# Choosing the 256 keys of sparse attention from the sign of score less threshold, on ScalarE

## The chip, the cores and the metric

The kernel runs on one core of a Trainium2 chip. The metric is device time in microseconds of one execution. The core has five engines that each work through a queue of their own in order: TensorE (PE, matmuls; PEld is its weight load), VectorE (DVE), ScalarE (ACT), GpSimd (POOL) and SyncE (SP, which issues DMA).

## The reference

Two layers, each with gated linear attention (4 heads) and sparse attention (8 heads) over 1040 tokens of width 1024. What matters here is the choice of keys:

```python
score = jnp.einsum('bqj,bqjs->bqs', iwb * (IDX_HEADS ** -0.5), jax.nn.relu(dots))
causal = key_pos[None, :] <= t[:, None]
score = jnp.where(causal[None], score, -jnp.inf)
_, sel = lax.top_k(score, topk)                    # topk = 256
...
s = jnp.where(valid[:, :, None, None, :], s, -jnp.inf)
p = jax.nn.softmax(s, axis=-1)
```

Each query keeps the 256 causal keys with the highest score. Of keys whose score equals the lowest one kept, those that come first are kept.

## The kernel before, in words

The kernel gathers no keys. It holds scores for a block of 128 queries on 128 partitions, in tiles `score[i]` for blocks 1 to 7 that are W = 144 + 128 i columns wide: 272, 400, 528, 656, 784, 912 and 1040, together 4592. Block 0 has at most 144 keys and needs no choice. For each query it finds the value of the 256th key (`sel_v`, one column for each block). From it, it makes a tile `bias[i]` in bfloat16 (in `r_kb`), 0 for a kept key and very large for any other, which L1023 adds to the attention scores S as it reads them from PSUM; the exponential (L1029, ScalarE) then follows.

The part that is changed (`cnt = er[0]` and the loop behind it) stands once in each layer's code. For each block, DVE counts the scores above the threshold (L866, with a sum in `cnt`), marks those equal to it (L867), runs a scan that numbers the equal ones from count - 256 on (L868), keeps the mark where the number is above 0, so that the place is too many (L870), and adds the scores below the threshold (L871). GpSimd multiplies by 1e30 (L872) and adds the causal mask for the last 128 columns (L873). The search for the threshold ends in a branch (L826 to L853) that all engines wait for and that is a longer search for rare cases.

Around the selection TensorE computes the gates of the two attentions, eight projections `proj_z` in three tiles of 348, 346 and 346 tokens. A tile is a group of 24 matmuls (L353 to L355, `wz`) into one PSUM bank. It is finished by three ScalarE passes (L404 to L406), one DVE pass (L731), an exponential (L732, ScalarE) and a product on DVE (L737) that is the last to read the bank and so frees it. Just behind the branch the values are transposed (L885, `vT`) and split into a high and a low part (`va`, `vb`: L887 ScalarE, L888 DVE), and the attention's keys `ak` are split likewise (L896, then L897). Then `stage_a` makes S (L1022, 144 columns for block 0, 272 for block 1), reads it (L1023) and takes the exponential; `stage_b` transposes the result (L1047, L1057) and multiplies by the values (L1053, L1054, L1063). Blocks 0 and 1 of this attention need no late `bias` tile, or only `bias[1]`; the others follow.

No queue is written by hand in full: a scheduler orders the instructions of each engine by a simulated time line when the program is built. So a change of one stage can move others.

Of the kernel before, what the change touches and what calls it, by code (L numbers as in the profile page):

```python
# [13 lines left out]
U8 = mybir.dt.uint8  # L14
U16 = mybir.dt.uint16
I16 = mybir.dt.int16
BF16 = mybir.dt.bfloat16
AF = mybir.ActivationFunctionType
OP = mybir.AluOpType
# [11 lines left out]
BIG = 1e30  # L31
# [65 lines left out]
def trunk(ctx: ExitStack, tc, a, out, dbg=None, stop=None):  # L97
# [58 lines left out]
    def small(n, dt=F32, parts=1):  # L156
        o = cofs[0]
        cofs[0] = o + n
        assert cofs[0] <= CST
        return cst[:, o:o + n].bitcast(dt) if dt != F32 else cst[:, o:o + n]  # L160
# [19 lines left out]
    V.memset(halves, 0.0)  # L180
    for o in range(2):
        V.memset(halves[64 * o:64 * o + 64, o:o + 1], 1.0)
    zcol = small(2)
    V.memset(zcol[:, 0:1], 0.0)
    V.memset(zcol[:, 1:2], 1.0)
    zero_b = zcol[:, 0:1]
# [222 lines left out]
    for l in range(DEPTH):  # L409
# [380 lines left out]
        with tc.high_priority(offset=TPRI):  # L790
# [65 lines left out]
                    V.drain()  # L856
                    finish(cnt, V.drain)

            cnt = er[0]
            for i in blks:  # L860
                W = 144 + 128 * i
                t = sel_v[:, i - 1:i]
                rr[5] = 1 - rr[5]
                oz = r_oz[:, rr[5]]
                eq, cs = oz[:, :260].bitcast(U8), oz[:, 260:780].bitcast(I16)
                V.tensor_scalar(bias[i], score[i], t, float(-TOPK), OP.is_gt, OP.add, accum_out=cnt[:, i - 1:i])  # L866
                V.tensor_scalar(eq[:, :W], score[i], t, None, OP.is_equal)  # L867
                V.tensor_tensor_scan(cs[:, :W], eq[:, :W], zero_b.to_broadcast([128, W]), cnt[:, i - 1:i],  # L868
                                     OP.add, OP.add)
                V.scalar_tensor_tensor(eq[:, :W], cs[:, :W], 0.0, eq[:, :W], OP.is_gt, OP.mult)  # L870
                V.scalar_tensor_tensor(score[i], score[i], t, eq[:, :W], OP.is_lt, OP.add)  # L871
                G.tensor_scalar(bias[i], score[i], BIG, 0.0, OP.mult, OP.add)  # L872
                G.tensor_tensor(bias[i][:, W - 128:W], bias[i][:, W - 128:W], causal[:, 16:144], OP.add)  # L873

        vat = [slot(1, F32R, "va"), slot(3, F32R, "vb")]
        va = []
# [305 lines left out]
def _tables():  # L1182
# [24 lines left out]
    for p in range(128):  # L1207
        for i in range(1, NB):
            nv = 17 + 128 * i + p
            z = NormalDist().inv_cdf(max(5e-3, 1 - TOPK / nv))  # L1210
            seltab[p, i - 1] = z
            seltab[p, 6 + i] = np.sqrt(2 * np.pi) / (nv * max(np.exp(-z * z / 2), 0.15))
            seltab[p, 13 + i] = BIG if nv >= TOPK else -BIG
            seltab[p, 20 + i] = nv >= TOPK
    seltab[:, 28:] = np.arange(8) + 0.5
    return {"ident": np.eye(128, dtype=np.float32), "causal": causal, "mcaus": mcaus, "lmask": lmask,
# [43 lines left out]
```

## Time and profile before

| | |
|---|---|
| median of 3 runs | 1513.29 us (1512.71 to 1514.68) |
| the profiled execution, whole | 1515.28 us |
| its span, first to last instruction | 1513.5 us |
| TensorE busy | 1386.8 us (92%) |
| DVE busy | 1061.5 us (70%) |
| ScalarE busy | 762.6 us (50%) |
| GpSimd busy | 723.3 us (48%) |
| mean granted TensorE clock | 0.965 |

The span is the profiled execution without what lies before its first and behind its last instruction, 1.8 us. Busy shares are averages over stages that have different limits; TensorE's matmuls are pipelined, so that its busy time is not its work at full speed. The granted clock is a share of 2.4 GHz; TensorE runs at this or at 1.2 GHz.

### The profile page before, as it was taken

The numbers are of one execution on the slowest core, as the hardware profiler recorded it, in microseconds if no ns is written. First come the engines' busy times: TensorE is split into PE (matmuls) and PEld (weight loads), VectorE is DVE, ScalarE is ACT, GpSimd is POOL, SyncE is SP. The second block draws the span as 40 slices with busy tenths as digits, with TensorE's granted clock in tenths as the row PEclk, the third lists the DMA queues.
The fourth block names the chain that finished last, engine by engine and source line by source line (L and its number), as shares of the span: only waits on it lengthen the run. The fifth ranks groups of instructions, "written<-read, shape, count | busy, mean of one in ns | idle before, by whom it ended". The sixth has DMA issues, their size and how long they took to land. (4 is left out here: it accounts for less than half of the span.)

```text
span 1513.5 us, 27140 instructions
## 1 busy us (share of the span) xinstructions
PE 1386.8 (92%) x9471; PEld 1290.6 (85%) x9471; DVE 1061.5 (70%) x2465; ACT 762.6 (50%) x1745; POOL 723.3 (48%) x690
## 2 busy tenths in 40 slices
PE   2988998999968999999999899999997899999985
PEld 2888897898958998898998889888897799899985
DVE  8569999565197556776497699994624955778638
ACT  5446623343355777653254573334434577876412
POOL 6533346596344546322363442866923644652134
PEclk9999999999978999999999999999998899999988
DMA  7242331242423446215233432314242253631422
GB/s 250 102 141 82 91 116 50 86 127 83 129 64 92 136 132 163 66 48 158 75 126 116 124 98 81 107 58 127 83 131 64 65 147 106 183 109 52 153 67 112
DMA packets 143166, 162.63 MB, mean 107 GB/s; under 512 B 19552, under 2 KB 112496, under 8 KB 143024
## 3 DMA queue, kind: packets, MB, share of 16 engines
q1 hardware_dynamic: 112656, 125.73, 27.9%
q10 hardware_dynamic: 30368, 35.12, 6.8%
q8 instruction: 75, 1.23, 0.3%
q14 instruction: 67, 0.55, 0.1%
HBM read 104.76 MB, written 56.04 MB: 106 GB/s over the span
## 5 line engine op out<-in xcount | busy, mean ns | idle before, releaser
L320 POOL TENSOR_TENSOR w<-w 128x512 fp32r<-128x512 f32 (+1 forms) x134 | 179.4, 1339 | 299.6 <-ACT w L319 232.5
L319 ACT ACTIVATE w<-w 128x512 fp32r<-128x512 f32 (+1 forms) x134 | 83.4, 624 | 108.7 <-DMA w<-in_w_fm_dram 58.4
L353 PE MATMUL wz<-X,w 128*128 128x346 f32 (+1 forms) x384 | 130.5, 340 | 2.3 <-DVE zu L737 1.8
L540 DVE SCALAR_TENSOR_TENSOR r_sc<-v,cst,r_sc 128x346 f32<-128x346 f32 (+6 forms) x196 | 125.0, 693 | 6.3 <-ACT v L535 5.2
L354 PE MATMUL wz<-X,w 128*128 128x346 f32 (+1 forms) x384 | 129.3, 337 | 0.0
L355 PE MATMUL wz<-X,w 128*128 128x346 f32 (+1 forms) x384 | 129.3, 337 | 0.0
L1051 DVE TENSOR_TENSOR u<-PT,u 128x512 fp32r<-128x512 f32 (+1 forms) x160 | 100.4, 632 | 30.1 <-ACT u L1050 21.3
L1050 ACT ACTIVATE u<-PT 128x512 fp32r<-128x512 f32 (+1 forms) x160 | 85.9, 544 | 61.9 <-PE PT L1047 60.4
L1029 ACT ACTIVATE r_g<-r_g,cst 128x272 f32<-128x272 f32 (+7 forms) x128 | 99.7, 779 | 20.1 <-DVE cst L1023 19.8
L632 POOL TENSOR_TENSOR qb<-r_g,u 64x256 f32<-64x256 f32 (+1 forms) x144 | 104.2, 724 | 5.8
L1022 PE MATMUL S<-ak,aq 128*128 128x346 f32 (+7 forms) x240 | 81.9, 348 | 18.8 <-DVE ak L897 10.3
L567 PE MATMUL gvp<-w,X 128*128 128x256 f32 (+1 forms) x288 | 83.3, 291 | 9.5 <-DVE r_g L643 8.0
L535 ACT ACTIVATE v<-dots 128x346 f32<-128x346 f32 (+5 forms) x224 | 85.8, 457 | 12.2 <-PE dots L533 8.5
L1047 PE MATMUL PT<-cst,r_g 128*128 128x128 f32 x576 | 89.2, 278 | 1.1 <-DVE cst L1023 1.1
L568 PE MATMUL gvp<-w,X 128*128 128x256 f32 (+1 forms) x288 | 83.4, 290 | 0.0
L569 PE MATMUL gvp<-w,X 128*128 128x256 f32 (+1 forms) x288 | 82.8, 288 | 0.0
L353 PEld LDWEIGHTS wz<-X,w 128*128 128x128 f32 x384 | 76.4, 199 | 3.9 <-DVE zu L737 2.3
L354 PEld LDWEIGHTS wz<-X,w 128*128 128x128 f32 x384 | 76.7, 200 | 0.3
L355 PEld LDWEIGHTS wz<-X,w 128*128 128x128 f32 x384 | 76.4, 199 | 0.4
L1117 PE MATMUL yp<-w,X 128*128 128x256 f32 (+1 forms) x238 | 69.9, 295 | 6.0 <-ACT X L1087 6.0
L643 DVE COPY_PREDICATED r_g<-cst,lev 128x512 f32<-128x512 uint8 (+1 forms) x72 | 52.5, 729 | 32.0 <-PE lev L639 31.4
L1022 PE MATMUL S<-ak 128*128 128x346 f32 (+7 forms) x240 | 74.8, 320 | 0.0
(348 smaller groups left out, 4900.6 us busy)
## 6 DMA issues: line engine op xcount, KB each, us to landing
w<-in_w_fm_dram SPq DMA_DIRECT2D x88, 256.0 KB
r_g<-aq_dram SPq DMA_DIRECT2D x64, 128.0 KB
w<-in_w_out_dram SPq DMA_DIRECT2D x32, 256.0 KB
r_sc<-h_dram SPq DMA_DIRECT2D x53, 128.0 KB
h_dram<-r_g SPq DMA_DIRECT2D x12, 512.0 KB
r_dram<-r_sc SPq DMA_DIRECT2D x48, 128.0 KB
r_sc<-z_dram SPq DMA_DIRECT2D x22, 256.0 KB
z_dram<-zu ACTq DMA_DIRECT2D x32, 173.0 KB
```

The source lines that it names most:

```text
L320: G.tensor_tensor(lo[:, :n], raw[:, :n], hi[:, :n].bitcast(F32), OP.subtract)
L353: T.matmul(p[:m, :n], wh, xh, start=(k == 0), stop=False)
L354: T.matmul(p[:m, :n], wh, xl, start=False, stop=False)
L355: mm = T.matmul(p[:m, :n], wl, xh, start=False, stop=(k == 7))
L535: S.activation(rl[:, :n], p[:, :n], AF.Relu)
L540: V.scalar_tensor_tensor(sco[:, c:c + n], rl[:, :n], w, sco[:, c:c + n], OP.mult, OP.add)
L632: eng.tensor_tensor(qb[P, :, o].rearrange("p c (b m) -> p c b m", m=m), qv[P, :, 1, :].rearrange("p (c b) m -> p c b m", c=nch), Ev[P, :, ...
L1022: mm = T.matmul(p[:, :n], q[x][:, h % 4, :], ak[g][:, c:c + n], start=(x == 0), stop=(x == 1))
L1029: ins = S.activation(P[:, :W], P[:, :W], AF.Exp, bias=mx[:, h, nci - 1:nci], scale=-1.0, accum_out=mx[:, h, 4:5]).ins
L1047: T.transpose(p[:, 256 * x + 128 * hh:256 * x + 128 * hh + 128], Pt[hh][:, 128 * (k0 + x):128 * (k0 + x) + 128], ident)
L1050: S.activation(ph[:, :256 * kk], p[:, :256 * kk], AF.Copy)
L1051: V.tensor_tensor(pl[:, :256 * kk], p[:, :256 * kk], ph[:, :256 * kk].bitcast(F32), OP.subtract)
```

## The change

ScalarE now takes the sign of score - threshold (`sg`, +1, 0 or -1, L867 of the new file) with its sum, and its square (`ne`, 1 where the score is not the threshold, L868) with its sum. The two sums give the number of keys above the threshold, and so the room for equal ones (`room`, two DVE operations on one column, L870 and L871). A scan on DVE counts the room down by one at each equal key (L872), 2048 times the sign is added (L873), and ScalarE's Relu with the scale -1e30 makes the bias (L874): a kept key ends at 0, any other far above it. The thresholds of queries with fewer than 256 keys are half as far from zero as before, so that masked scores stay below them, and the causal mask is not added any more. Scans and marks are held in 16 bits where they were in 8 and 16.

```diff
--- before.py
+++ after.py
@@ -180,7 +180,8 @@
     V.memset(halves, 0.0)
     for o in range(2):
         V.memset(halves[64 * o:64 * o + 64, o:o + 1], 1.0)
-    zcol = small(2)
+    zcol = small(3)
+    V.memset(zcol[:, 2:3], -1.0)
     V.memset(zcol[:, 0:1], 0.0)
     V.memset(zcol[:, 1:2], 1.0)
     zero_b = zcol[:, 0:1]
@@ -856,21 +857,21 @@
                     V.drain()
                     finish(cnt, V.drain)
 
-            cnt = er[0]
+            negt, sums, room = sel_w[10], sel_w[8:10], sel_w[7]
+            V.tensor_scalar(negt, sel_v, -1.0, BIG / 2, OP.mult, OP.min)
             for i in blks:
-                W = 144 + 128 * i
-                t = sel_v[:, i - 1:i]
+                W, x = 144 + 128 * i, slice(i - 1, i)
                 rr[5] = 1 - rr[5]
-                oz = r_oz[:, rr[5]]
-                eq, cs = oz[:, :260].bitcast(U8), oz[:, 260:780].bitcast(I16)
-                V.tensor_scalar(bias[i], score[i], t, float(-TOPK), OP.is_gt, OP.add, accum_out=cnt[:, i - 1:i])
-                V.tensor_scalar(eq[:, :W], score[i], t, None, OP.is_equal)
-                V.tensor_tensor_scan(cs[:, :W], eq[:, :W], zero_b.to_broadcast([128, W]), cnt[:, i - 1:i],
-                                     OP.add, OP.add)
-                V.scalar_tensor_tensor(eq[:, :W], cs[:, :W], 0.0, eq[:, :W], OP.is_gt, OP.mult)
-                V.scalar_tensor_tensor(score[i], score[i], t, eq[:, :W], OP.is_lt, OP.add)
-                G.tensor_scalar(bias[i], score[i], BIG, 0.0, OP.mult, OP.add)
-                G.tensor_tensor(bias[i][:, W - 128:W], bias[i][:, W - 128:W], causal[:, 16:144], OP.add)
+                sg, oz = bias[i], r_oz[:, rr[5]]
+                left, ne = oz[:, :520].bitcast(I16), oz[:, 520:].bitcast(BF16)[:, :W]
+                S.activation(sg, score[i], AF.Sign, bias=negt[:, x], scale=1.0, accum_out=sums[0][:, x])
+                S.activation(ne, sg, AF.Square, accum_out=sums[1][:, x])
+
+                V.tensor_scalar(room[:, x], sums[0][:, x], sums[1][:, x], -0.5, OP.add, OP.mult)
+                V.tensor_scalar(room[:, x], room[:, x], float(TOPK), None, OP.add)
+                V.tensor_tensor_scan(left[:, :W], ne, zcol[:, 2:3].to_broadcast([128, W]), room[:, x], OP.add, OP.add)
+                V.scalar_tensor_tensor(left[:, :W], sg, 2048.0, left[:, :W], OP.mult, OP.add)
+                S.activation(bias[i], left[:, :W], AF.Relu, scale=-BIG)
 
         vat = [slot(1, F32R, "va"), slot(3, F32R, "vb")]
         va = []
@@ -1210,7 +1211,7 @@
             z = NormalDist().inv_cdf(max(5e-3, 1 - TOPK / nv))
             seltab[p, i - 1] = z
             seltab[p, 6 + i] = np.sqrt(2 * np.pi) / (nv * max(np.exp(-z * z / 2), 0.15))
-            seltab[p, 13 + i] = BIG if nv >= TOPK else -BIG
+            seltab[p, 13 + i] = BIG if nv >= TOPK else -BIG / 2
             seltab[p, 20 + i] = nv >= TOPK
     seltab[:, 28:] = np.arange(8) + 0.5
     return {"ident": np.eye(128, dtype=np.float32), "causal": causal, "mcaus": mcaus, "lmask": lmask,
```

**The built order.** Names are those of the tiles, out<-in, with sizes; lines of the new file are one higher than those of the old one from line 184 on. In ScalarE's queue of the first layer, this is what stands right behind the branch before, from the last pass of the z tile in hand to the weights, values and keys:

```order
L406 ACTIVATE zu<-zu,cst 128x348
L404 ACTIVATE zu<-wz 128x346
L405 ACTIVATE zu<-zu 128x346
L406 ACTIVATE zu<-zu,cst 128x346
L319 ACTIVATE w<-w 128x512
L887 ACTIVATE va<-vT 128x8x64
L887 ACTIVATE va<-vT 128x2x64
L887 ACTIVATE vb<-vT 128x6x64
L887 ACTIVATE vb<-vT 16x2x64
L896 ACTIVATE ak<-r_g 128x1040 x2
L396 ACTIVATE ak<-r_g 128x512 x2
```

Of the new queue, the branch and that z pass are followed by the seven Signs, of which the last two stand here, and by this:

```order
L867 ACTIVATE r_kb,cst<-r_sc,cst 128x912
L867 ACTIVATE r_kb,cst<-r_sc,cst 128x1040
L405 ACTIVATE zu<-wz 128x346
L733 ACTIVATE zu<-zu 128x348
L868 ACTIVATE r_oz,cst<-r_kb 128x272
L868 ACTIVATE r_oz,cst<-r_kb 128x400
L320 ACTIVATE w<-w 128x512
L888 ACTIVATE va<-vT 128x8x64
L888 ACTIVATE va<-vT 128x2x64
L888 ACTIVATE vb<-vT 128x6x64
L888 ACTIVATE vb<-vT 16x2x64
L897 ACTIVATE ak<-r_g 128x1040 x2
```

The Signs and two Squares stand in front of the values and the keys, and the second and third z tiles behind them; the other Squares and the Relus are spread over what follows.

In DVE's queue of the first layer, these rows come first behind the branch before:

```order
L866 TENSOR_SCALAR r_kb,cst<-r_sc,cst 128x272
L867 TENSOR_SCALAR r_oz<-r_sc,cst 128x272
L866 TENSOR_SCALAR r_kb,cst<-r_sc,cst 128x400
L867 TENSOR_SCALAR r_oz<-r_sc,cst 128x400
L866 TENSOR_SCALAR r_kb,cst<-r_sc,cst 128x528
L866 TENSOR_SCALAR r_kb,cst<-r_sc,cst 128x656
L866 TENSOR_SCALAR r_kb,cst<-r_sc,cst 128x784
L866 TENSOR_SCALAR r_kb,cst<-r_sc,cst 128x912
L866 TENSOR_SCALAR r_kb,cst<-r_sc,cst 128x1040
L731 SCALAR_TENSOR_TENSOR zu<-wz,zu 128x348
L868 SCALAR_TENSOR_TENSOR r_oz<-r_oz,cst 128x272
L868 SCALAR_TENSOR_TENSOR r_oz<-r_oz,cst 128x400
```

and these now:

```order
L861 TENSOR_SCALAR cst<-cst 128x7
L732 SCALAR_TENSOR_TENSOR zu<-wz,zu 128x348
L738 TENSOR_TENSOR zu<-wz,zu 128x348
L870 TENSOR_SCALAR cst<-cst 128x1
L871 TENSOR_SCALAR cst<-cst 128x1
L870 TENSOR_SCALAR cst<-cst 128x1
L872 SCALAR_TENSOR_TENSOR r_oz<-r_oz,cst 128x272
L871 TENSOR_SCALAR cst<-cst 128x1
L873 SCALAR_TENSOR_TENSOR r_oz<-r_kb,r_oz 128x272
L872 SCALAR_TENSOR_TENSOR r_oz<-r_oz,cst 128x400
L889 TENSOR_TENSOR va<-vT,va 128x8x64
L889 TENSOR_TENSOR va<-vT,va 128x2x64
```

The seven counts are gone from the front, and the product that frees the first z tile's bank (L737, now L738) has come up from behind the keys to the third place.

In TensorE's queue of the first layer, the first S tiles (numbers tell tiles apart) stand behind the first of the z groups that follow the branch (`wz_5044`) and ahead of the second (`wz_5077`):

```order
L355 MATMUL wz_5044<-X_90,w_5040 128x348
L1022 MATMUL S_4863<-ak_4839,aq_4848 128x144
L1022 MATMUL S_4863<-ak_4839 128x144
L1022 MATMUL S_4868<-ak_4839,aq_4848 128x144
L1022 MATMUL S_4868<-ak_4839 128x144
L1022 MATMUL S_4984<-ak_4839,aq_4848 128x144
L1022 MATMUL S_4984<-ak_4839 128x144
L353 MATMUL wz_5077<-X_90,w_5033 128x346
L354 MATMUL wz_5077<-X_90,w_5033 128x346
```

Now all of the second group, 24 matmuls (`wz_5079`, of which the last stands here), comes before S, and the S tiles of all eight heads come together:

```order
L356 MATMUL wz_5079<-X_91,w_5042 128x346
L1023 MATMUL S_4865<-ak_4841,aq_4850 128x144
L1023 MATMUL S_4870<-ak_4841,aq_4850 128x144
L1023 MATMUL S_4986<-ak_4841,aq_4850 128x144
L1023 MATMUL S_4865<-ak_4841 128x144
L1023 MATMUL S_4870<-ak_4841 128x144
L1023 MATMUL S_4986<-ak_4841 128x144
L1023 MATMUL S_4991<-ak_4841,aq_4850 128x144
L1023 MATMUL S_4991<-ak_4841 128x144
L1023 MATMUL S_5002<-ak_4841,aq_4850 128x144
L1023 MATMUL S_5002<-ak_4841 128x144
```

The second layer has the same order in all three places. The rest of the program differs only in small exchanges between neighbours.

## Rows read from the trace of the kernel before

**Rows 1.** The page's 40 slices: busy tenths of DVE, TensorE's granted clock.

```profile
DVE  8569999565197556776497699994624955778638
...
PEclk9999999999978999999999999999998899999988
```

**Rows 2.** Busy times by stretch: TensorE, weights, DVE, ScalarE, GpSimd, then clock.

```profile
419.20:466.30 47.10, 31.70 (x157) 29.08 (x158) 46.98 (x87) 24.80 (x66) 28.04 (x22) 0.71 0.24 71
1154.40:1200.10 45.70, 33.41 (x157) 31.00 (x158) 43.49 (x82) 24.99 (x66) 24.55 (x20) 0.71 0.24 69
...
430.00:440.00 10.00, 6.54 (x23) 6.37 (x24) 9.94 (x25) 4.08 (x13) 2.68 (x5) 0.50 0.31 101
```

**Rows 3.** TensorE's waits, first layer, 400 to 500: us, times, longest.

```profile
PE S L1022 <- DVE cst L1023: 5.7, 2, 5.1
PE S L1022 <- DVE ak L897: 5.0, 1, 5.0
```

**Rows 4.** TensorE's longest wait, second layer, 1136 to 1236.

```profile
PE S L1022 <- DVE ak L897: 5.3, 1, 5.3
```

**Rows 5.** Groups by line: the selection's passes, both layers (busy us, mean ns).

```profile
L868 DVE TENSOR_TENSOR_SCAN r_oz<-r_oz,cst 128x272 int16<-128x272 uint8 (+6 forms) x14 | 25.6, 1859 | 0.0
...
L870 DVE SCALAR_TENSOR_TENSOR r_oz<-r_oz 128x272 uint8<-128x272 int16 (+6 forms) x14 | 16.2, 1172 | 0.1
...
L871 DVE SCALAR_TENSOR_TENSOR r_sc<-r_sc,cst,r_oz 128x272 f32<-128x272 f32 (+6 forms) x14 | 14.2, 1027 | 0.0
L872 POOL TENSOR_SCALAR r_kb<-r_sc 128x272 bf16<-128x272 f32 (+6 forms) x14 | 12.4, 883 | 35.4 <-DVE r_sc L871 35.0
...
L866 DVE TENSOR_SCALAR_CACHE_REDUCE r_kb<-r_sc,cst 128x272 bf16<-128x272 f32 (+6 forms) x14 | 11.9, 890 | 17.2 <-PE vT L885 9.7 <-DVEq L828 7.5
...
L873 POOL TENSOR_TENSOR r_kb<-r_kb,cst 128x128 bf16<-128x128 bf16 x14 | 10.5, 750 | 1.0
...
L867 DVE TENSOR_SCALAR r_oz<-r_sc,cst 128x272 uint8<-128x272 f32 (+6 forms) x14 | 10.0, 726 | 0.0
```

**Rows 6.** ScalarE's groups by form.

```profile
L1029 ACT ACTIVATE r_g<-r_g,cst 128x1040 f32<-128x1040 f32 x16 | 18.5, 1157 | 2.0 <-DVE cst L1023 2.0
...
L405 ACT ACTIVATE zu<-zu 128x346 f32<-128x346 f32 x32 | 15.5, 486 | 1.1 <-DVE zu L737 0.6
...
L896 ACT ACTIVATE ak<-r_g 128x1040 fp32r<-128x1040 f32 x4 | 4.0, 1054 | 0.0
...
L107 ACT ACT_TABLE_LOAD x1 | 1.3, 1283 | 0.7 <-PEq L1249 0.7
```

**Rows 7.** TensorE's timeline, first layer: start, length, idle before.

```profile
423.53 0.32 PE L353 MATMUL wz<-X,w 128*128 128x348 f32 x1
...
427.20 0.33 PE L355 MATMUL wz<-X,w 128*128 128x348 f32 x1
...
432.54 0.46 PE L1022 MATMUL S<-ak,aq 128*128 128x144 f32 x1 [5.01 <-DVE ak L897]
...
434.99 0.66 PE L353 MATMUL wz<-X,w 128*128 128x346 f32 x1 [0.93 <-DVE zu L737]
...
460.90 0.66 PE L353 MATMUL wz<-X,w 128*128 128x348 f32 x1
...
466.27 0.32 PE L353 MATMUL wz<-X,w 128*128 128x346 f32 x1
```

**Rows 8.** DVE's timeline, first layer: splits of values and of keys.

```profile
429.59 0.87 DVE L888 TENSOR_TENSOR va<-vT,va 128x512 fp32r<-128x512 f32 x2
430.39 0.73 DVE L888 TENSOR_TENSOR vb<-vT,vb 128x384 fp32r<-128x384 f32 x2
431.15 2.39 DVE L897 TENSOR_TENSOR ak<-r_g,ak 64x1040 fp32r<-64x1040 f32 x2
```

**Rows 9.** DVE's groups by form.

```profile
L731 DVE SCALAR_TENSOR_TENSOR zu<-wz,zu 128x346 f32<-128x346 f32 x32 | 16.4, 511 | 11.7 <-ACT zu L406 8.9 <-PE o L1053 2.5
...
L1023 DVE CUSTOM_DVE_ANT_0 r_g<-S,cst 128x144 f32<-128x144 f32 x16 | 4.1, 298 | 0.0
```


## The prediction, made before the changed kernel was run

> **What bounds the kernel now.** I read the 40 slices first. The granted clock of TensorE (PEclk) is 9 tenths or more in nearly every slice, and dips to 7 and 8 in slices 12 and 13, to 8 in 31 and 32, and at the very end [rows 1]. DVE is at 9 in slices 12 and 32, where the two layers select their keys. So I asked for the busy times from the moment when all engines come out of the selection's branch to the end of the fourth group of 24 z matmuls (`wz`) behind it on TensorE's queue: 47.1 us in the first layer (to 466.27 [rows 7]), 45.7 us in the second [rows 2]. In the first, DVE is busy 47.0 of 47.1 us; TensorE only 31.7, at 0.71 of its clock; ScalarE 24.8; GpSimd 28.0. DVE fills this stage and TensorE waits for it. In the slices around it the clock is full, which I read as TensorE setting the pace there; so time gained here is kept unless something else stops it.
>
> The waits of TensorE say for what [rows 3]: 5.7 us for S tiles that the masked score pass (L1023) still had to read, 5.0 us for the split of the attention keys (L897). In the second layer it is 5.3 us for L897 [rows 4]. (There is also a wait at the branch itself, which the change leaves alone.) Each such gap is paid twice: in the 10 us around the 5.0 us gap the granted clock is 0.50 [rows 2], that is 1.2 GHz. A group of 24 z matmuls takes 3.8 us at the full clock (423.53 to the end of the one at 427.20) and 5.4 us when it starts at the low one (460.90 to 466.27) [rows 7].
>
> **What the change removes, adds and moves.** Off DVE, for a layer (half of each line's total) [rows 5]: the counting compare L866 6.0 us, the equality L867 5.0, the product L870 8.1; of L871 7.1 us one pass of the same form stays (`sg` x 2048 + `left`, same widths). The scan L868 stays, 12.8 us. Added are 14 one-column operations and one of seven; no row has such a pair, so they lie between nothing and the 0.3 us of a 144-column L1023 [rows 9]; I take 0.1 each, as they are the smaller kind, 1.5 us in all (0 to 4.5). DVE loses 19.1 - 1.5 = 17.6 of its 47 us. GpSimd loses L872 and L873, 11.5 us a layer; TensorE hardly waits for it here, so I cost that at nothing.
>
> ScalarE gains 21 passes over 4592 columns each. Copying 1040 columns takes 1.054 us and 346 take 0.486, so a column is 0.82 ns and the fixed part 0.20; with a bias column, 1040 take 1.157 us, so 0.30 fixed [rows 6]. Sign: 4592 x 0.82 ns + 7 x 0.30 = 5.9 us. Square and Relu: 3.8 + 7 x 0.20 = 5.2 us each. Together 16.3 us, on an engine that is idle for 22 of 47 us here.
>
> The Trainium skill speaks against such a move: its page "ScalarE: Activation LUTs" (section "Rules for kernel authors") gives relu and products to VectorE, which it calls up to about 3x faster in bf16. By that, Square and Relu would cost a third on DVE, an estimate of 3.4 us in place of 10.4, and the change would overload ScalarE. The rows of this case do not agree: L871 averages 1.03 us where the mean width is 656 columns, 1.6 ns a column [rows 5], against 0.82 for ScalarE [rows 6].
>
> How the sum of busy times turns into time depends on the new order, so I walked the rows of the three queues, from the release of the branch as 0, with L numbers of before.
>
> Keys. ScalarE's queue now has the seven Signs ahead of everything (0.5 to about 6.4), then two z passes (0.49 each), two Squares (1.0), a weight (0.6), the four value copies (some 1.6, as DVE's splits of the same tiles) and only then the two key copies (2.1): done at about 12, with starts that overlap a little. DVE, with its seven counts gone, waits for its first Square until 7.7 and then does two scans (672 of 4592 columns of 12.8 us: 1.9), two passes of L871's kind (1.0), the value splits (0.87 + 0.73) and L897 (2.39 for two, S needs the first) [rows 8]: S can begin at about 13.8, against 432.54 - 419.2 = 13.3 before [rows 7]. No gain there by itself. But the second group of 24, which stood behind the S tiles, and started at 434.99 after another 0.93 us of waiting [rows 7], now stands in front. Its PSUM bank is free at 7.7, when DVE's L737 for the first z tile runs, which came just before 434.99. It fills 8.3 (427.5, where the first group ends before) to 12.1 at full clock, and the gap shrinks from 5.0 to about 2 us.
>
> Third group. From its last L897 at 15.0, DVE does eight L1023 at 0.3, the scans of 528 and 656 columns (3.3), two L871-like passes (1.8), three z passes at 0.51 [rows 9] and some 0.5 of small ones: L737 frees this group's bank at 24.5. ScalarE must have done some 38 passes by then: 12 z passes 5.9 us, seven Signs 5.9, four Squares 2.3, two Relus 0.95, six of 512 columns 3.7, key copies 2.1, value copies 1.6, five exponentials 2.1, end to end 24.5, and since consecutive passes overlap a little, 21 to 24. It is close behind DVE, no further. [...]
>
> Fourth group. DVE goes on with a 272-column L1023 (somewhat over 0.3, 0.4), scans of 784 and 912 (4.7), two passes (2.6), z passes (1.0), the small ones and two remainder passes (1.3): 34.5. That also covers the bank of the fourth group. The attention matmuls follow to 35.1, then the group of 24 in 5.4: 40.5. These scans are averages that include some beside GpSimd work, which shrinks; I take 40. Before, the same point came at 47.1 and 45.7 [rows 2], and the second layer has the same new order. Gain: 7.1 + 5.7 = 12.8 us.
>
> Against the profiled execution's 1515.28 us (span 1513.5 and 1.8 around it) that gives 1502.5. The median of the runs is 1513.29, 2.0 lower, so **1500.5, say 1501 us**.
>
> **Rivals.** A change of 0.2% (3 us) is what a measurement of this kernel can tell from none.
>
> *ScalarE takes DVE's place, and it gets slower.* The needed passes (the copy of the keys, the exponentials L1029, the z passes L732 that free banks) stand behind Signs, Squares and Relus in one queue. ScalarE now has 24.8 + 16.3 = 41.1 us in a stage that I want to be 40 long, though part of the Relus comes after the last landmark. If it keeps 8 us of waiting for DVE out of the 22 that it has now, the stage lasts 49: 2 and 3 us longer than before, 1513.3 + 5 = 1518. It decides from the point where ScalarE is more than 7 us late at the fourth group. For it: the margin at the third is under 3 us. Against it: from the Signs on the order leaves ScalarE almost no item that must wait long. It is also how the page's rule would show itself.
>
> *DVE was all that counted.* If ScalarE never holds anyone, the stage is DVE's remaining 47.0 - 17.6 = 29.4 us plus some waits at its start, say 33: 14 + 13 = 27 us, 1486. For it: DVE was 47.0 of 47.1 busy. Against it: DVE idles until the first Square at 7.7.
>
> *The waits only change names.* S begins no earlier than before, and TensorE may lose behind it what the moved group gains, or later in the layer: within 3 us of 1513. Against it: the fourth group ends 6 to 7 us earlier by rows.
>
> *Sign is in another function table.* One load took 1.28 us [rows 6]; switching there and back would cost 2.6 us a layer, 1506. The built order shows the one load at the program's start and no other, so this has little chance.
>
> **How the numbers follow.** Forecast with its own range 1494 to 1508: 0.65 (the table case within it). More gain, 1480 to 1494: 0.12. Names only, 1508 to 1516: 0.13. ScalarE late, above 1516: 0.10. The range that leaves out less than 2 in 10 is 1489 to 1514: outside lie the lower half of the second case, the last one, and some 0.03 of the third. Faster by over 0.2% (below 1510.3): 0.65 + 0.12 + 0.04 of the third = 0.81; within: 0.08; slower: the remaining 0.01 of the third and the last, 0.11.
>
> **What would show it.** DVE's busy total falls from 1061.5 by about 35 us, ScalarE's rises by about 32, GpSimd's falls by about 23. Right after the branch: seven Signs back to back from 0.51 to about 1.16 us; 24 z matmuls without a gap before the first S; that S at about 14 us, no earlier than now. The stage to the end of the fourth group is near 40 us in both layers, at a clock above 0.71. Wrong, if TensorE's waits there sum to as much as now under ScalarE's lines; if Sign or Square take clearly more than L1029 at their width; if the scan, which now reads bf16 for uint8, or the passes over int16 are slower than L868 and L871; or if TensorE waits later in the layer for as long as it gained.

## The result, and the profile after

The changed kernel is **slower**: 1524.58 us (median of 7 runs, 1521.49 to 1532.69) against 1513.46 (7 runs), a ratio of 1.0071, 95% interval 1.0046 to 1.0096. Forecast were 1501 us and a range of 1489 to 1514. Its profiled execution has a span of 1519.7 us, 6.2 more than before. In it DVE's busy total fell by 26.6 us to 1034.9 (35 were forecast), ScalarE's rose by 30.2 to 792.8 (32), GpSimd's fell by 19.2 to 704.1 (23). So the work moved much as forecast, and the time did not follow. Of the page's 40 slices, DVE's and the granted clock's, as in [rows 1]:

```profile
DVE  8569999564175556775587799984723745777638
...
PEclk9999999999979999999999999999998799999998
```

In slices 12 and 32 DVE is at 7 where it was at 9, and the clock still dips there.

The stage from the release of the branch to the end of the fourth group of z matmuls behind it, first and second layer, columns as in [rows 2]:

```profile
418.93:464.90 45.97, 31.70 (x156) 29.00 (x156) 37.29 (x75) 38.94 (x99) 16.48 (x10) 0.74 0.27 79
1157.49:1205.42 47.93, 34.05 (x156) 30.96 (x156) 36.91 (x75) 39.09 (x99) 16.50 (x10) 0.69 0.27 80
```

It was to take 40 us and takes 46.0 and 47.9, against 47.1 and 45.7 before [rows 2]. Over the whole stretch DVE is no longer full (37 us), ScalarE is now the busiest with 39, and TensorE works as long as before at about the same clock. But DVE's idle time lies almost all at the start: the product of the first z tile waits for an exponential (L733) that stands behind the seven Signs in ScalarE's queue. From this row to the end of the product for the fourth group DVE is full again, 32.0 of 32.7 us (its row, then the two parts of the stretch, columns as above):

```profile
426.00 0.52 DVE L738 TENSOR_TENSOR zu<-wz,zu 128x348 f32<-128x348 f32 x1 [5.99 <-ACT zu L733]
```

```profile
418.93:426.00 7.07, 7.07 (x37) 6.99 (x38) 0.64 (x2) 7.07 (x18) 0.00 (x0) 0.76 0.13 33
426.00:458.70 32.70, 18.48 (x96) 16.08 (x94) 31.95 (x65) 29.20 (x78) 15.38 (x10) 0.76 0.32 94
```

TensorE's waits in the first layer's stretch (us, times, longest) answer to [rows 3]; the one for vT is the branch:

```profile
PE wz L354 <- DVE zu L738: 4.5, 2, 2.8
PE vT L886 <- DVEq L829: 4.2, 1, 4.2
PE S L1023 <- DVE ak L898: 4.1, 1, 4.1
PE PT L1048 <- ACT zu L407: 1.9, 1, 1.9
PE S L1023 <- DVE cst L1024: 1.8, 1, 1.8
PE o L1054 <- DVE u L1052: 1.5, 1, 1.5
PE PT L1048 <- DVE zu L738: 0.5, 1, 0.5
```

Without the branch these are 14.3 us; before, they were 15.3. The two large names of [rows 3] have shrunk from 5.7 and 5.0 to 1.8 and 4.1, and in their place stand 4.5 us for products of z (L738), 1.9 for a z pass of ScalarE (L407) and smaller ones. In the second layer the split of the keys holds S for 4.5 us, where it was 5.3 [rows 4]:

```profile
PE S L1023 <- DVE ak L898: 4.5, 1, 4.5
```

The selection's passes by line, both layers, answer to [rows 5]:

```profile
L872 DVE TENSOR_TENSOR_SCAN r_oz<-r_oz,cst 128x272 int16<-128x272 bf16 (+6 forms) x14 | 23.1, 1648 | 0.4
...
L873 DVE SCALAR_TENSOR_TENSOR r_oz<-r_kb,r_oz 128x272 int16<-128x272 bf16 (+6 forms) x14 | 17.6, 1259 | 0.1
...
L867 ACT ACTIVATE r_kb<-r_sc,cst 128x272 bf16<-128x272 f32 (+6 forms) x14 | 11.6, 828 | 1.4 <-DVE cst L861 1.4
...
L874 ACT ACTIVATE r_kb<-r_oz 128x272 bf16<-128x272 int16 (+6 forms) x14 | 10.3, 738 | 2.5 <-DVE r_oz L873 2.2
L868 ACT ACTIVATE r_oz<-r_kb 128x272 bf16<-128x272 bf16 (+6 forms) x14 | 10.3, 734 | 0.0
```

In the tables below a **stage** goes from the end of a layer's first group of 24 z matmuls to the end of its seventh, which is the fourth behind the branch in most kernels; **between** goes from the last z matmul of layer 0 to the end of the first group of layer 1. Both are read from TensorE's timeline by counting z matmuls. The expectations count stages from the branch (46.0 for 56.2) or from the second group (some 4 us less than from the first), and the stretch between to the second branch or to the second group of layer 1.

Of the 6.2 us between the two profiled spans, the first stage has -1.2, the second +2.2, the stretch between +3.1; the z matmuls behind the stages have +1.4 and +0.3, the rest +0.4. The forecast was -12.8, all of it in the stages: of the 19 us between forecast and profile, the stages have 13.8 and the rest of the program 5.2.

### The profile page after: what moved, and what is told of

It is laid out like the page before. It is cut to its first block, busy times and chain, and to the rows that moved or that the text cites. A ratio compares the mean times of both kernels' runs of the same rounds, so it can differ in the third digit from the quotient of the medians.

```text
span 1519.7 us, 27197 instructions
## 1 busy us (share of the span) xinstructions
PE 1395.3 (92%) x9471; PEld 1296.5 (85%) x9471; DVE 1034.9 (68%) x2440; ACT 792.8 (52%) x1815; POOL 704.1 (46%) x662
## 5 line engine op out<-in xcount | busy, mean ns | idle before, releaser
L399 POOL TENSOR_TENSOR aq<-r_g,aq 64x512 fp32r<-64x512 f32 x32 | 42.2, 1318 | 71.8 <-ACT aq L397 45.2
```

## The experiments

Each ratio is to runs of the kernel before on the same chip, with its 95% interval. That kernel's own median went from 1513.5 to 1518.6 us in the five comparisons, so ratios are compared, not times. The span is that of one run, and not always a typical one: the profiled runs of the changed kernel and of e14 are the fastest of their runs, those of e2, e6 and e7 the slowest.

| run | ratio | span, us | stage 0 | stage 1 | between |
|---|---|---|---|---|---|
| before | | 1513.5 | 57.5 | 56.1 | 585.8 |
| changed | 1.0071 (1.0046 to 1.0096) | 1519.7 | 56.2 | 58.3 | 588.9 |
| e1 changed again | 1.0047 (1.0029 to 1.0064) | 1521.4 | 58.0 | 58.5 | 589.2 |
| e2 new in layer 0 | 1.0053 (1.0034 to 1.0071) | 1530.3 | 56.4 | 61.4 | 595.6 |
| e3 new in layer 1 | 1.0013 (0.9995 to 1.003) | 1518.1 | 57.3 | 59.6 | 588.1 |
| e4 Square, Relu on DVE | 0.9931 (0.991 to 0.9951) | 1504.6 | 50.9 | 50.5 | 584.1 |
| e5 keys first | 0.9925 (0.9906 to 0.9943) | 1502.8 | 48.6 | 48.5 | 585.0 |
| e6 Relu on DVE | 0.9988 (0.9975 to 1.0) | 1518.9 | 54.5 | 55.8 | 589.5 |
| e7 old tail | 0.9957 (0.9942 to 0.9971) | 1514.0 | 50.8 | 49.9 | 587.0 |
| e8 before again | 1.0004 (0.999 to 1.0019) | 1516.5 | 58.4 | 55.5 | 588.5 |
| e9 old, order between as changed | 1.0012 (1.0 to 1.0024) | 1514.5 | 59.8 | 53.8 | 588.3 |
| e10 old, keys first | 1.0092 (1.0073 to 1.0112) | 1528.2 | 56.4 | 56.7 | 601.4 |
| e11 keys first, Relu on DVE | 0.9948 (0.9932 to 0.9965) | 1506.0 | 49.8 | 50.5 | 584.8 |
| e12 two blocks, keys, five blocks | 0.9929 (0.9915 to 0.9944) | 1502.7 | 45.7 | 55.7 | 585.7 |
| e13 one product first | 0.9929 (0.99 to 0.9957) | 1508.2 | 53.7 | 52.9 | 585.1 |
| e14 keys and products first | 0.9929 (0.9901 to 0.9956) | 1497.4 | 46.4 | 46.4 | 584.2 |

**One profile against another (e1, e8).** Both kernels unchanged.

> The changed kernel once more, for a second profile and more times. Its seven runs went from 1521.5 to 1532.7 us, where those of before went from 1512.6 to 1518.6, and the profiled one was the lowest, 6.2 us of span above before. Theory (the loss is fixed by the order of the queues): the stretches agree with the first profile within 0.5 us each, stage of layer 0 about 46.0 us, stage of layer 1 about 47.9, the stretch from 540 us to the second branch 3.2 us above before, and the median stays near 1524. Rival (the loss is mostly a wait that differs from run to run): one or two stretches outside the stages differ by 2 us or more between the two profiles.

> The kernel before with one blank line more, for a second profile of it on the chip of these runs, where its median was 1518.3 us in place of 1513.3. Theory A (one order of the queues gives one length of each stretch, but for waits on loads): stages 47 and 46 us, 688 us from the fourth group to the second branch, within 2 us each; what the span has over 1513.5 lies at one to three places where a load from DRAM lands late. Rival: the stretch between the layers is 3 or more us longer here too, and then it does not tell the two orders apart.

One kernel's stretches agree within about 2 to 3 us, not 0.5: e1's first stage is 1.8 us longer than in the first profile, e8's stretch between the layers 2.7. Differences of that size in one profile therefore say nothing by themselves; the ratios decide.

**One layer at a time (e2, e3).** `if l == 0:` or `if l == 1:` ahead of the new loop, the old one behind `else:`.

> The new selection in the first layer alone, the old one in the second. Theory A (the selection stage is neutral in layer 0, and what is lost in the middle of the program comes from queues that the scheduler put in another order there): fourth group of the first layer 46 us behind the branch, +3 us between 540 us and the second branch, the second stage as before at 45.7: span 1516.5, ratio about 1.002. Theory B (the selection itself costs the time, by a late key or bank in the stage): the second branch comes at its old place within 1 us, and the span is 1513 to 1514, since layer 0's stage was no longer than before.

> The old selection in the first layer, the new one in the second. Theory A (reordered queues outside the stage): nothing is lost up to the second branch (1154.4 within 1 us), the stage is 47.9 us long, 2.2 over before, and some 1 us more is lost behind it: span 1516.5, ratio 1.002. Theory B (the stage costs the time wherever it stands): the same in the second layer, so the two theories differ here only in what they say of the stretch before it; if the second branch comes 3 us late although layer 0 is as before, both are wrong.

By the ratios nearly the whole loss comes with the first layer's selection (8 us, where the changed kernel loses 7 to 11), although its stage is not longer. In e2's profile the stretch between has 595.6 us; the second stage with its 61.4 us holds the old passes, so its length is not theirs; what makes it so long stays open. Theory B falls for layer 0, but theory A's numbers (span 1516.5, ratio 1.002) are missed too. e3 is too near to 1 to tell. Its second branch comes 2.8 us late, at 1157.2 us, which its expectation would count against both theories; but e8, the kernel before unchanged, has it at 1157.4.

**What ScalarE's load costs (e4, e6, e7).**

```diff
-S.activation(ne, sg, AF.Square, accum_out=sums[1][:, x])                          # e4
+V.tensor_scalar(ne, sg, 0.0, 0.0, OP.not_equal, OP.add, accum_out=sums[1][:, x])  # e4
-S.activation(bias[i], left[:, :W], AF.Relu, scale=-BIG)                           # e4, e6
+V.tensor_scalar(bias[i], left[:, :W], -BIG, 0.0, OP.mult, OP.max)                 # e4, e6
```
```diff
-V.scalar_tensor_tensor(left[:, :W], sg, 2048.0, left[:, :W], OP.mult, OP.add)     # e7
-S.activation(bias[i], left[:, :W], AF.Relu, scale=-BIG)
+V.scalar_tensor_tensor(left[:, :W], left[:, :W], 0.0, ne, OP.is_lt, OP.is_gt)
+V.scalar_tensor_tensor(score[i], sg, 0.0, left[:, :W], OP.is_lt, OP.add)
+G.tensor_scalar(bias[i], score[i], BIG, 0.0, OP.mult, OP.add)
```

> Square and Relu moved from ScalarE to VectorE as a compare with sum and a multiply with max, the Signs stay. Theory A (ScalarE's queue is what holds the keys and the z passes): ScalarE loses 10.4 us a layer, S starts 1 to 2 us earlier (the Squares of 272 and 400 columns stand ahead of the keys now, 0.9 us), the fourth group 2 to 4 us earlier than in the changed kernel, span 1512 to 1516. Theory B (DVE is still the bound behind the keys): each pass costs 1.3 us or so on DVE as its add with the sign does, some 12 us a layer more on it, the fourth group 5 or more us later, span above 1527. The Trainium skill (ScalarE: Activation LUTs, Rules for kernel authors) gives such passes to VectorE, up to about 3x faster in bf16: by an estimate of it 3.4 us in place of 10.4, which would be theory A's side.

> Only the Relu moved to DVE; Sign and Square stay on ScalarE. Its queues between the layers stand as in the changed kernel. By the rows of the run with both passes moved, the pass costs DVE 0.35 us at 784 columns where GpSimd is idle and 1.1 us at 912 beside a GpSimd pass, some 3 to 5 us a layer, and relieves ScalarE of 5.2. Theory A (order between the layers): stretch from the fourth group to the second branch 693 us as in the changed kernel although the stage is shorter. Theory C (ScalarE's load bounds the stage): fourth group at 43, half way from 46.0 to 40.5, in both layers: with A a span of 1513 to 1515. If C is wrong and the Square's place ahead of DVE's scans matters, the stage stays at 45 to 46: 1519.

> Sign and Square with their sums on ScalarE as in the change, the end as before: DVE marks the keys that are too many, adds the sign's negative, GpSimd multiplies by 1e30; no Relu, no causal addition. Queues between the layers as in the kernel before. ScalarE has 5.2 us a layer less than in the changed kernel, DVE some 7 more, GpSimd some 9 more. Theory C (ScalarE's load): stage at 43. Theory D (DVE passes beside GpSimd passes cost two to three times as much, as the add of 272 columns did with 1.35 us against 0.44): GpSimd is busy during most of DVE's adds, DVE's stage grows to 47 or more, as before. Theory A (order between the layers) expects 688 us from the fourth group to the second branch. A and D: span 1513 to 1516; A and C: 1507 to 1509.

e4 and e7 shorten the stages by 5 to 8 us and end 0.7% and 0.4% below the kernel before; e6, which takes as much load off ScalarE as e7, shortens them by 2 to 3 and ends at 0.9988. Counted from the branch, e6's stages are 44.1 and 42.9 us, near the 43 of theory C. In e7 the z matmuls behind the stages take 2 to 4 us longer than in the changed kernel. e4 came out below both of its theories and e7 with shorter stages than C or D gave it. In e4 S starts later than in the changed kernel, 19.1 us behind the branch and not 16.2, and the stage is shorter all the same. So neither load alone nor the first S explains these runs; each of them also has another order of the queues. What e4's rows do show is that DVE has work, 1.1 us behind the branch, in the 6 us in which it waits in the changed kernel; it is then busy for 39.8 of 40.5 us:

```profile
419.81 0.43 DVE L868 TENSOR_SCALAR_CACHE_REDUCE r_oz<-r_kb 128x272 bf16<-128x272 bf16 x1
```

**Another order, the same passes (e5, e10).** The lines from `vat = ...` to the split of `ak` stand ahead of the selection's loop, in e5 of the new and in e10 of the old one:

```diff
+vat = [slot(1, F32R, "va"), slot(3, F32R, "vb")]
+...
+V.tensor_tensor(ak[g][64:128], raw[64:128], ak[g][64:128].bitcast(F32), OP.subtract)
 for i in blks:
```

> All three new ScalarE passes stay; the code of the values and keys (vT, va, vb, ak) is written ahead of the selection's loop. In the built queues the Signs still stand first on ScalarE, but DVE now splits values and keys behind the first block's scan and add, ahead of the second's; and the queues between the layers (720 to 1100 us) stand as in the kernel before, where the changed kernel has them in another order. Theory A (order between the layers costs the changed kernel 4 to 5 us): the stretch from the end of the first layer's fourth group to the second branch is 688 us as before (735.2 - 47.3), not 693 as in the changed kernel. Theory B (keys are late because of what stands in front of them on DVE): S starts 2 to 3 us earlier than 16.2 behind the branch and the fourth group ends 2 to 3 earlier, at 43 to 44. Theory C (ScalarE's 41 us are the bound): fourth group at 46 or later whatever the keys do. A and B together give a span near 1508, A with C 1513, C alone 1518 to 1520.

> The old selection with the code of the values and keys written ahead of it: the order of the run that gained 12 us, without the change. Theory E (the gain of that run is the earlier keys and the better order, and the new passes add little): from the second to the seventh z group 45 to 48 us in place of 53.4, span 1505 to 1509. Theory F (the gain needs the 17.6 us a layer that the new passes take off DVE): 51 to 54 us as before, 1512 to 1516. The queues between the layers have a third order here, so the stretch between the layers may differ by 3 us either way.

e5 keeps all 21 passes a layer on ScalarE and is 0.75% faster than the kernel before; its stages are 48.6 and 48.5 us long. The branch comes 3 us later there, and from it the seventh group ends at 35.4 and 35.6 us; so it is not ScalarE's load that holds the changed kernel's at 46 or later (theory C). In this shorter stage, though, ScalarE is full, 34.8 of 35.4 us (columns as in [rows 2]):

```profile
421.68:457.12 35.44, 26.29 (x134) 24.38 (x135) 28.84 (x63) 34.79 (x93) 14.26 (x9) 0.77 0.34 98
```

With the old passes the same edit leaves the stages at 56.4 and 56.7, as theory F had it: in this order the stage becomes short only with what the change takes off DVE. e10 also shows what an order elsewhere can cost: it loses 13 to 16 us between the layers, where none of its work is different.

**The order between the layers (e9).** The kernel before, with 16 seven-column operations on DVE (`if l == 0: V.tensor_scalar(sel_w[10], sel_v, -1.0, BIG / 2, OP.mult, OP.min)`, 16 times) ahead of its loop, and nothing of the change.

> The kernel before with nothing of the change: only 16 operations on seven columns are added to DVE in layer 0, ahead of the selection. They shift the scheduler's time line, and its queues between the layers come out in the changed kernel's order and not in that of before. They cost DVE 1.5 to 3 us in the first stage (0.1 to 0.2 each). From the last z matmul of layer 0 to the end of the second group of z matmuls of layer 1, four kernels with the order of before took 588.2 to 592.5 us in six profiles, three with the changed kernel's order 592.9 to 599.7 in four. Theory A (order between the layers): 593 to 596 here, and a span of 1518 to 1522. Rival (that stretch is longer because of something that the new passes leave behind, or by chance): 588 to 592, span 1515 to 1518.

Its TensorE has between the layers the wait that marks the changed kernel's order, and that no kernel with the order of before has (TensorE's waits of the changed kernel, then of e9):

```profile
PE go L668 <- DVE r_g L644: 5.4, 1, 5.4
```

```profile
PE go L667 <- DVE r_g L643: 5.1, 1, 5.1
```

Ten profiles with the order of before have 584.1 to 588.5 us between (middle 585.4), five with the changed kernel's 588.3 to 595.6 (middle 589.2). But e9's stretch lies on the border between its two theories (592.3 us as counted there), e9 as a whole is 1.0012 (1.0 to 1.0024) of before, and two profiles of before differ by 2.7. So this order costs 0 to 4 us; how much was not settled. The wait of 5.4 us is a mark and not that cost: TensorE's waits between the layers sum to 19.7 us in the changed kernel and 21.8 before.

**Two blocks first, and the Relu with early keys (e12, e11).** e12 runs the loop for blocks 1 and 2, then the code of the keys, then the loop for the others; e11 is e5 with the Relu line of e6.

> The changed kernel with the loop of the selection split: blocks 1 and 2 first, then the code of values and keys, then blocks 3 to 7. Order between the layers as before. By the trace of the changed kernel the fourth z group waited for a product on DVE that stood behind the scan of 1040 columns; here the late blocks come behind the keys and may be spread further back. If that wait is what cost the changed kernel its gain, the second to seventh group take 45 us or less and the span is 1500 to 1506. If it was the lateness of S (16.2 us behind the branch), which two scans and two adds ahead of the keys keep, it stays at 50 to 52 and 1513.

> The changed kernel with the code of values and keys first, and the Relu on DVE as a multiply and max. Order between the layers as before. If ScalarE's load still counts once the order is good (theory C), the 5.2 us a layer taken from it shorten the stage from 44.8 to 43 or less, span 1499 to 1502. If it does not, the 3 to 5 us a layer that DVE gets instead show: 46 to 48 us, span 1505 to 1508.

e12 comes out at 45.7 us in one layer and 55.7 in the other, with the same code but with queues in different orders; its span of 1502.7 is that of its first theory. e11's stages are 1 to 2 us longer than e5's and its ratio is higher, but the two intervals overlap: that the Relu is cheaper on ScalarE than on DVE in this order is likely, not shown.

**One row moved (e13, e14).**

```diff
+zp = V.tensor_tensor(e[:, :n], p, e[:, :n], OP.mult).ins; zn[0] += 1
+for x in zh.pop(zn[0], ()): hold(x, zp.name)
...
+scan = V.tensor_tensor_scan(left[:, :W], ...)
+if i == 7: zh.setdefault(4, []).append(scan.ins)
```

> The changed kernel with one constraint in each layer: the scan of 1040 columns may start only behind the fourth product of z (L738 on a 348-column tile). In the first layer's DVE queue of the stage only these two change places; the queues between the layers come out in the order of before. Theory G (the fourth z group's bank behind that scan is a part of the missing gain): the group starts 2.4 us earlier in each layer (scan 2.38), the stage to its end is 43 to 44 us in layer 0 and 45 to 46 in layer 1, span 1514 to 1516 with the changed kernel's order between the layers, 1512 to 1515 with that of before. Theory H (DVE has as much to do, what is gained at this group is lost at the next): the fourth group comes earlier but the span stays at 1519 to 1521.

> The changed kernel with the code of the keys first and the scans of 656, 784 and 912 columns held behind the third, fourth and fifth product of z. In the run with keys first TensorE still waited 3.0 us in each layer for such a product behind an add of 656 columns, and 2.5 us for the first one. Theory G: that wait of 3.0 us goes in both layers, from the first to the seventh group 45 to 46 us in place of 48.6, span 1496 to 1501. Theory H: the late scans are then late for the attention of the later blocks, TensorE waits for them behind the seventh group, span 1502 to 1506.

DVE and TensorE at the fourth group in the changed kernel: the product waits for the scan, the group for the product.

```profile
455.91 2.38 DVE L872 TENSOR_TENSOR_SCAN r_oz<-r_oz,cst 128x1040 int16<-128x1040 bf16 x1
...
458.21 0.49 DVE L738 TENSOR_TENSOR zu<-wz,zu 128x348 f32<-128x348 f32 x1
...
458.75 0.66 PE L354 MATMUL wz<-X,w 128*128 128x348 f32 x1 [2.83 <-DVE zu L738]
```

The same place in e13:

```profile
454.41 0.51 DVE L739 TENSOR_TENSOR zu<-wz,zu 128x348 f32<-128x348 f32 x1
...
454.84 2.37 DVE L874 TENSOR_TENSOR_SCAN r_oz<-r_oz,cst 128x1040 int16<-128x1040 bf16 x1
...
454.97 0.43 PE L354 MATMUL wz<-X,w 128*128 128x348 f32 x1 [0.44 <-DVE zu L739]
```

The gap of 2.83 us is 0.44, the first stage is 2.5 us shorter as theory G had it, the second 5.4. Its busy times and its clock (first and second layer, columns as above, from the branch to the end of the fourth group):

```profile
417.61:461.02 43.41, 31.61 (x156) 28.64 (x156) 36.27 (x74) 38.46 (x98) 16.48 (x10) 0.76 0.28 80
1148.60:1191.49 42.89, 30.97 (x155) 28.19 (x155) 35.54 (x74) 38.46 (x98) 16.25 (x10) 0.77 0.28 82
```

The ratio falls from 1.0071 and 1.0047 to 0.9929. Of the 11.5 us between the profiled spans the two stages give 7.9; between the layers, where e13 has the order of before, its profile has 3.8 less than the changed one's. By the ratios the gap is 18 to 21 us; what the profiles don't show of it stays open. More than one row differs in e13: the order between the layers too, and a wait in the second layer (below). Every kernel that gained 0.4% or more has the order of before between the layers; e9 puts that order at 4 us at most, so it is not the whole gap. In e14 the wait of 3.0 us is 1.1 and the stages are 46.4 us as theory G had it, 2.1 to 2.2 shorter than e5's; but the z matmuls behind them take 2.2 and 2.5 us longer, which is theory H. The ratios of e14, e13, e12 and e5 are all 0.7% below the kernel before, and none can be told from another.

## Why the prediction was wrong, point by point

**What bounds the kernel: right.** DVE held TensorE up in the stage, and most of what is won there is kept: e5's two stages are 16.4 us shorter than before, its span 10.7.

**Prices of the passes: mostly right.** Sign 0.51 to 1.15 us and Square and Relu 5.2 us a layer came as reckoned (11.6, 10.3 and 10.3 us for both layers, and some 0.2 more each to read a sum). The scan got slightly cheaper (1648 ns for 1859). Wrong was the pass "of L871's kind": 1259 ns instead of 1027, and 2.8 us instead of 1.0 for the two narrow ones that stand ahead of the keys. The one-column operations take 0.13 to 0.21 us where 0.1 was taken. The passes listed under "Third group" are 42, not 38; their sum is right.

**The step "Keys": S at 16.2 us, not 13.8.** DVE's and GpSimd's rows of the changed kernel, first layer, and TensorE's S:

```profile
427.87 1.35 DVE L873 SCALAR_TENSOR_TENSOR r_oz<-r_kb,r_oz 128x272 int16<-128x272 bf16 x1
...
431.36 1.45 DVE L873 SCALAR_TENSOR_TENSOR r_oz<-r_kb,r_oz 128x400 int16<-128x400 bf16 x1
...
433.03 4.24 DVE L898 TENSOR_TENSOR ak<-r_g,ak 64x1040 fp32r<-64x1040 f32 x2
```

```profile
427.55 1.38 POOL L321 TENSOR_TENSOR w<-w 128x512 fp32r<-128x512 f32 x1 [13.10 <-ACT w L320]
431.11 2.83 POOL L399 TENSOR_TENSOR ak<-r_g,ak 64x512 fp32r<-64x512 f32 x2 [2.18 <-ACT ak L397]
434.88 1.29 POOL L321 TENSOR_TENSOR w<-w 128x512 fp32r<-128x512 f32 x1 [0.95 <-ACT w L320]
```

```profile
435.18 0.53 PE L1023 MATMUL S<-ak,aq 128*128 128x144 f32 x3 [4.08 <-DVE ak L898]
```

The add of 272 columns takes 1.35 us and ends 0.3 behind the end of GpSimd's w at 428.93; the add of 400 takes 1.45; the two key splits take 4.24 us where they took 2.39 [rows 8], and S, which needs the first of them, starts 1.2 us behind the end of GpSimd's second `ak` at 433.94. Where GpSimd is idle, in e4, the 272-column add takes 0.44 (below). What these DVE operations have in common in the code is that both their inputs lie in SBUF. The Trainium skill says it ("SBUF — State Buffer", section "Who interferes with whom"): a DVE instruction with two SBUF inputs contends with a GpSimd instruction that reads SBUF. These rows agree. The prediction set GpSimd's share at nothing because TensorE hardly waits for it, and did not ask what GpSimd does beside these rows of DVE. The adds cost 1.8 us too much and the first key split, by itself 2.00 us where it took 1.24, 0.8: 2.6 together, where S is 2.4 us late.

```profile
433.03 2.00 DVE L898 TENSOR_TENSOR ak<-r_g,ak 64x1040 fp32r<-64x1040 f32 x1
```

**The step "Fourth group": its bank came at 39.8, not 34.5.** This is the step that failed by most. I wrote that 34.5 "also covers the bank of the fourth group", with scans of 784 and 912 columns in the sum. The product that frees this bank stands behind the scan of 1040 columns as well, 2.4 us. Another 2.6 us were there already when the third group started (27.1 for 24.5): by DVE's rows the two adds are 1.8 us over the sum and the two key splits 1.9, while the first product comes 0.6 early (7.1 for 7.7). The group then takes 6.2 us where 5.4 were reckoned. e13 shows the part of the scan in the first layer: with scan and product exchanged, the group starts 0.44 us and not 2.83 behind the matmuls ahead of it.

**"The second layer has the same new order": true of the rows, not of the times.** There the first operation of DVE behind the branch waits for the last transpose of the values, 2.0 us behind it, before and after. Before, ScalarE did not depend on it; now its Signs need `negt`:

```profile
1159.51 0.17 DVE L861 TENSOR_SCALAR cst<-cst 128x7 f32<-128x7 f32 x1 [9.70 <-PE vT L886]
```

```profile
1159.71 0.52 ACT L867 ACTIVATE r_kb<-r_sc,cst 128x272 bf16<-128x272 f32 x1 [1.41 <-DVE cst L861]
```

So S starts at 18.0 us. What this costs the stage is not shown: in e3 and e13 the wait is not there and S starts at 16.2 us, but e3's stage from the branch is only 0.8 us shorter (47.1 for 47.9). In e13 it may be part of the 5.4 us.

**No term for the rest of the program.** The sum assumed that other stretches stay as they are, and the text ahead of the prediction calls the differences there small exchanges between neighbours. But the queues of the next 600 us come out in another order, marked by the wait of 5.4 us: 0 to 4 us here, 13 to 16 in e10.

**The rivals.** "ScalarE takes DVE's place" has the right sign, but its condition, ScalarE late at the fourth group, did not come: the exponential for that product ends at 453.48, 4.7 us before the product. Of TensorE's 14.3 us only 1.9 carry a ScalarE line, and e5 runs all passes there. ScalarE's part is DVE's 6.0 us of waiting behind the Signs, which the forecast had ("until 7.7"; it was 7.1). The page of the Trainium skill named beside this rival ("ScalarE: Activation LUTs", section "Rules for kernel authors") holds for one of the two passes: the Relu of 784 columns takes 0.84 us on ScalarE and 0.35 on DVE in e4. The page gives its factor for operations with one source; L871, by which the prediction set the rule aside, has two. Beside a GpSimd pass the Relu of 912 columns took 1.10 us on DVE, the Square gains nothing there (1040 columns: 1.22 us in e4, 1.05 on ScalarE), and moving the Relu did not help in e11. "The waits only change names" is what happened in the stages (15.3 us to 14.3). "DVE was all that counted" is near in kind and far in size: DVE is full from 7.1 us on, but had 37 us of work where this rival had 29.4. No table load was added.

**What follows.** The change saves what it was said to save, but not in the order that the scheduler makes of it. With the keys' code moved ahead or with one product held in front of the last scan, it is worth 0.7%; as it stands it costs 0.5 to 0.7%. That the wait for the product costs the first stage its 2.5 us is shown by e13's rows; how its further gain divides between the second layer's wait, the stages' clock and the order between the layers is not.

## What to carry to other kernels

Busy time taken off the engine that bounds a stage is only an offer. Walk the new queue down to the operation that frees each buffer TensorE waits for, by its row and not by its line, and name everything in front of it; a transfer to another engine also changes what runs beside the operations that stay. Where a scheduler builds the order, run the change in two or three orders before judging it, since the same passes gave ratios from 0.993 to 1.007 here.

## What the runs showed of the hardware that I had not expected

A DVE operation with two SBUF inputs is not slowed in proportion when it meets a GpSimd pass; in these rows it ends a little less than its own time behind the end of that pass. With GpSimd idle, the adds of 272 and 400 columns and a key split take 0.44, 0.57 and 1.24 us in e4:

```profile
421.97 0.44 DVE L873 SCALAR_TENSOR_TENSOR r_oz<-r_kb,r_oz 128x272 int16<-128x272 bf16 x1
...
424.04 0.57 DVE L873 SCALAR_TENSOR_TENSOR r_oz<-r_kb,r_oz 128x400 int16<-128x400 bf16 x1
...
436.46 1.24 DVE L898 TENSOR_TENSOR ak<-r_g,ak 64x1040 fp32r<-64x1040 f32 x1
```

In the changed kernel's first layer the same adds end 0.29 and 0.43 us behind the GpSimd operation that they meet, and both key splits 1.10. (The profile's spans on GpSimd are rough.)

The Relu on DVE in e4 has one SBUF input and looks the same: 784 columns with GpSimd idle, then 912 beside a GpSimd pass from 453.09 to 454.37, behind which it ends by 0.26 us.

```profile
452.24 0.35 DVE L874 TENSOR_SCALAR r_kb<-r_oz 128x784 bf16<-128x784 int16 x1
...
453.53 1.10 DVE L874 TENSOR_SCALAR r_kb<-r_oz 128x912 bf16<-128x912 int16 x1
```
